# Weight sums made ahead that stand later on VectorE, and a last quarter of the down projection that makes its sums in place

## The chip, the cores and the metric

The kernel runs on one core of a Trainium2 chip. A core has a TensorE (PE) for matmuls, a VectorE (DVE) and a ScalarE (ACT) for elementwise work, a GpSimd (POOL), and a SyncE (SP) that issues most of the DMAs. The metric is the device time of one execution in microseconds (us); the time given is the median of several runs. A profile is one execution taken by the hardware profiler, whose times are a little longer than the median.

## The reference

One layer of a hybrid encoder on 512 tokens of width 2048, in float32:

```python
xn = _rmsnorm(h, norm_mix[l])
y = xn @ w_in[l]
o_gdn = _gdn_group(y[..., :GDN_COLS], ...)
o_rwkv = _rwkv_group(y[..., GDN_COLS:], ...)
h = h + concat([o_gdn, o_rwkv]) @ w_out[l]
h = h + _cross_attention(_rmsnorm(h, norm_xattn[l]), _rmsnorm(mem, norm_mem[l]), ...)
hn = _rmsnorm(h, norm_mlp[l])
h = h + jnp.square(jax.nn.relu(hn @ mlp_w_up[l])) @ mlp_w_down[l]
return _rmsnorm(h, norm_final)
```

The change concerns the last product, the down projection: 512 tokens, 8192 rows of weights, 2048 columns. Part of the change is also felt in the mixers (the two groups `gdn` and `rwkv`), because work for the down projection is done there as a filler.

## The kernel before, in words

**Stages.** In order of time: the input projection and the mixers (to about 1100 us), the output projection and the cross-attention (to about 1700), the up projection with 32 units (to about 2334), and the down projection with 8 units (to about 2944), then the last norm and the stores.

**Precision.** Every weight tile is cut in two by `cut` (line 1775): ScalarE copies it to a rounded half `whi`, VectorE subtracts to get the rest `wlo`. Three products of halves (high by high, low by high, high by low) replace one float32 product. There are three pairs of halves (`hfree`), so a cut can be at most three tiles ahead of the matmuls.

**Seven products for eight.** Output, up and down projections multiply 2 by 2 blocks with seven products instead of eight. Beside the four weight blocks A11, A12, A21, A22 that needs four sums: s1 = A21 + A22, s2 = s1 - A11, s3 = A11 - A21, s4 = A12 - s2. In the order of `order_of` (line 1803) a down unit multiplies A11 (product B11), A12 (B21), s2 (T2), s1 (T1), s3 (T3), s4 (B22) and A22 (T4). The right sides are blocks of the squared activations, made by `activations` (line 2131).

**Down.** A unit `("d", e, m)` has 2048 of the 8192 rows (e from 0 to 3) and one of two column groups (m). It runs the seven products, each over x = 0 to 3, that is four tiles of 128x1024; a tile is 12 matmuls of 512 columns. `downout` (line 2067) adds each finished product, for each of two token blocks t, from PSUM into the result rows `H`; two products into one bank follow each other only when the first has been added (the event "snap"). When e = 3, `final` (line 2164) follows: the squares for the last norm, and the product with its gain `wf`.

**Sums made ahead.** For the up projection the sums are made on the spot (`adds`). For down they are made ahead, in groups `(e, m)` of `GROUPS` (line 383), 16 in all, where e now counts 1024 rows: `presum` (line 391) loads a piece of the four blocks to four tiles, makes the four sums in place on VectorE, and stores each to DRAM (`Sd`). In the mixers, `presums` runs it in pieces of 410 columns on one set of four tiles `ds` (`NSET`, `PIECE`, `PRANK`, line 387) until the event `("kp", 15)`. What is left is done in chunks of 512 by `remaining` and `leftover` (lines 2191 and 2199): in up on the tiles of `abfree` until `("ud", 26, 1)`, and in down on the tiles of `cfree`. A group is 4 loads and 4 stores of a megabyte each, and later 4 more megabytes of loads of its sums. `loads` (line 1781) loads a down unit's tiles in the order of the products; a tile of a sum waits until its group is stored.

**Order.** The stages concerned are scheduled by hand. Generators (`chain`) yield one operation after another, and `run` (line 284) picks, again and again, the operation with the earliest planned start; 150 ns per rank are added to that start, so a lower rank goes first. The planned start comes from `start` and `issue`, which keep a clock for each engine, the planned time at which each buffer's last write lands (`landed`) and its last reader ends (`seen`). A DMA lands 2.9 us or more after its issue by the plan, plus a `margin` that a `Lane` carries (line 197). What is picked is written to that engine's program at once, so the plan sets the fixed order of every engine's program, and an engine runs its own program in that order whatever the real times are.

**Buffers.** `wfree` holds six tiles of 128x1024 for weights, three tagged `wraw` and three `w2` (shown as w in the profile). Two tiles `ws` and two `ab` (128x1024 each) serve the sums in up and the activations later (`abfree`, eight halves). `cfree` holds three tiles `sl` and the tile `acc`, 512 columns each. `hp` holds the residual; `hp[7]` is free once the last rows of `H` have been transposed (`norm_`, `turned_`, line 2059). `finals` (line 2211) loads the gain of the last norm, `nf`, into the two `ab` tiles when all activations have been made.

## Time and profile before

| | us |
|---|---|
| median of 3 runs | 2950.43 (2950.02 to 2954.77) |
| the profiled execution's own time | 2957.76 |
| its span, first to last instruction | 2955.7 |
| PE busy in the span | 2886.4 (98%) |
| DVE busy | 2317.0 (78%) |
| ACT busy | 1573.5 (53%) |
| mean granted clock of PE | 0.994 |
| moved by DMA | 587.64 MB, 199 GB/s on average |

A profile names an instruction by the line that issued it, its engine and operation, and by "out<-in" in the program's names, with buffer numbers left out. Almost all instructions of the stages concerned carry line 256, since `issue` emits them, so one goes by the names: `ds` is a piece of the sums made ahead in the mixers, `py` the input projection, `gn`, `ri..`, `gpo` and `gi..` are small matmuls of the mixers, `whi` and `wlo` the halves of a weight tile, `h` the result rows, `mxd`, `mmd`, `mgd`, `scrd`, `scgd` PSUM banks of down, `cb` the cut blocks of activations. Waits are written as "engine name <- engine name of what ended the wait: total us, times, longest us". Rows of stages give the stage, its length, and the busy time of each engine in it with the number of instructions. In the order of time, a row is start, duration, engine, instruction, and in brackets the idle time ahead of it and what ended it.

### The profile page before, as it was taken

To read this page: it belongs to the slowest core of one execution; us is meant where nothing else is said; L and a number is where in the kernel's file an instruction comes from. 1 tells how busy PE (TensorE), PEld (TensorE's weight loads), DVE (VectorE), ACT (ScalarE), POOL (GpSimd) and SP (SyncE) were. 2 spreads that over 40 slices of the span, in tenths; PEclk is the share of its full clock that TensorE was granted. 3 is DMA by queue.
4 is the path that set the end of the run, shared out by engine and by line. 5 is a ranking of instruction groups with operands and counts; after the bars stand their busy time and mean duration, and the time that the engine had idled before them with its cause. 6 is when DMAs were issued, how large, how long until landed. Compare 5 with 4: busy or idle time off the path is not lost. (4 is left out here: it accounts for less than half of the span.)

```text
span 2955.7 us, 49493 instructions
## 1 busy us (share of the span) xinstructions
PE 2886.4 (98%) x18794; PEld 2428.0 (82%) x18794; DVE 2317.0 (78%) x3559; ACT 1573.5 (53%) x2233; POOL 232.0 (8%) x547
## 2 busy tenths in 40 slices
PE   9999999999999999999999999999999999999998
PEld 7777777777777878888998888888888888888886
DVE  7787786877877876768975898888898878787865
ACT  7454544554555645565444656555555645454544
POOL 0213213122132200000000000000000000000000
PEclk9999999999999999999999999999999999999999
DMA  5756757667666778786433244555555778988755
GB/s 189 210 172 183 204 166 203 188 171 206 179 196 176 218 240 288 233 267 218 138 98 92 89 160 153 175 176 174 182 187 181 245 241 275 311 263 296 249 193 171
DMA packets 338206, 587.64 MB, mean 199 GB/s; under 512 B 103016, under 2 KB 202604, under 8 KB 337968
## 3 DMA queue, kind: packets, MB, share of 16 engines
q1 hardware_dynamic: 311728, 555.12, 61.0%
q10 hardware_dynamic: 26240, 29.37, 2.9%
q8 instruction: 147, 2.41, 0.3%
q14 instruction: 91, 0.75, 0.1%
HBM read 465.47 MB, written 118.89 MB: 198 GB/s over the span
## 5 line engine op out<-in xcount | busy, mean ns | idle before, releaser
L256 ACT CAST whi<-wraw 128x1024 fp32r<-128x1024 f32 (+1 forms) x374 | 392.0, 1049 | 423.1 <-PE py L256 147.4
L256 DVE TENSOR_TENSOR wlo<-wraw,whi 128x1024 fp32r<-128x1024 f32 (+1 forms) x374 | 459.3, 1229 | 113.9 <-ACT whi L256 104.1
L256 PE MATMUL py<-xhi,whi 128*128 128x512 f32 x928 | 374.1, 403 | 6.4 <-ACT xhi L256 6.4
L256 PE MATMUL py<-xlo,whi 128*128 128x512 f32 x928 | 378.2, 408 | 0.0
L256 PE MATMUL py<-xhi,wlo 128*128 128x512 f32 x928 | 376.5, 406 | 0.0
L256 ACT CAST whi<-w 128x1024 fp32r<-128x1024 f32 x190 | 200.1, 1054 | 222.7 <-PE mxu L256 47.4
L256 DVE TENSOR_TENSOR wlo<-w,whi 128x1024 fp32r<-128x1024 f32 x190 | 231.7, 1221 | 64.2 <-ACT whi L256 63.7
L256 PE MATMUL mxu<-cb,whi 128*128 128x512 f32 x1016 | 255.0, 392 | 0.0
L256 DVE TENSOR_TENSOR ds<-ds,ds 128x410 f32<-128x410 f32 (+1 forms) x228 | 134.3, 589 | 99.7 <-DMA ds<-in_w_dm 95.4
L256 PEld LDWEIGHTS py<-xhi,whi 128*128 128x128 f32 x928 | 177.0, 191 | 42.2 <-ACT xhi L256 6.4
L256 PEld LDWEIGHTS mxu<-cb,whi 128*128 128x128 f32 x1016 | 182.8, 189 | 32.7
L256 PEld LDWEIGHTS py<-xlo,whi 128*128 128x128 f32 x928 | 176.9, 191 | 36.4 <-DVE xlo L256 0.8
L256 PEld LDWEIGHTS py<-xhi,wlo 128*128 128x128 f32 x928 | 177.0, 191 | 33.5 <-issue 1.0
L131 DVE TENSOR_TENSOR wlo<-wraw,whi 128x1024 fp32r<-128x1024 f32 x112 | 136.7, 1222 | 45.1 <-ACT whi L130 44.0
L130 ACT CAST whi<-wraw 128x1024 fp32r<-128x1024 f32 x112 | 117.7, 1052 | 87.2 <-PE op L122 24.7
L256 PEld LDWEIGHTS mxu<-cb,wlo 128*128 128x128 f32 x1016 | 138.7, 190 | 10.5 <-DVE wlo L256 0.7
L256 PE MATMUL mxu<-cb,wlo 128*128 128x256 f32 x1016 | 142.2, 282 | 0.3 <-DVE wlo L256 0.3
L256 PE MATMUL mgu<-cb,whi 128*128 128x512 f32 x512 | 129.4, 394 | 1.8 <-ACT whi L256 1.8
L256 ACT ACT_TABLE_LOAD x87 | 111.6, 1283 | 36.6 <-DVE suml_gn L256 21.2
L256 PE MATMUL mxd<-whi,cb 128*128 128x512 f32 x512 | 126.8, 389 | 0.0
L256 PE MATMUL mgd<-whi,cb 128*128 128x512 f32 x512 | 126.4, 389 | 0.0
L122 PE MATMUL op<-ob,whi 128*128 128x256 f32 (+1 forms) x752 | 115.3, 304 | 0.3 <-ACT whi L130 0.3
(921 smaller groups left out, 6555.7 us busy)
## 6 DMA issues: line engine op xcount, KB each, us to landing
wraw<-in_w_in SPq DMA_DIRECT2D x116, 512.0 KB, 5.0
ds<-in_w_dm SPq DMA_DIRECT2D x184, 205.0 KB, 4.1
sd_s<-ds SPq DMA_DIRECT2D x184, 205.0 KB, 4.3
wraw<-in_w_up SPq DMA_DIRECT2D x65, 512.0 KB, 3.6
w<-sd_s SPq DMA_DIRECT2D x65, 512.0 KB, 5.0
w<-in_w_up SPq DMA_DIRECT2D x63, 512.0 KB, 4.1
wraw<-sd_s SPq DMA_DIRECT2D x63, 512.0 KB, 5.4
wraw<-in_w_dm SPq DMA_DIRECT2D x49, 512.0 KB, 4.8
```

Of the source, the lines that this page charges most:

```text
L122: PE.matmul(o, l, r, start=start, stop=stop, skip_group_check=again)
L130: S.copy(hi, src)
L131: V.tensor_tensor(out=lo, in0=src, in1=hi.bitcast(F32), op=ALU.subtract)
L256: f(*a, **k)
```

## The change

Three edits belong together. `presum` issues its loads through a lane with a margin of 5000 ns, and the filler's rank goes from 4 to 5. The four groups of the last quarter, `INSITU`, are no longer made ahead: `GROUPS` has 12 groups. The last quarter of down, e = 3, runs as four units of two x each instead of two units of four; their four blocks are loaded raw and a new generator `insitu` makes the sums in place in the load buffers, with one buffer more for s1. `splits`, `multiply_` and `downout` follow the shorter range `xs(u)`. To hold ten load buffers, `finals` hands the `ab` and `ws` tiles to `wfree` once the activations are done, and the gain `nf` goes to `hp[7]` and two tiles of `cfree` as four loads of 512 columns. What is left of the sums is in up also made on `hp[7]`, in chunks of 256 columns, until `("ud", 30, 1)`.

```diff
@@ -380,21 +380,23 @@
         wq += [("s", mem4[j]) for j in range(4) if n == NSQ[j]]
         wq += [("w", I["w_in"][n][:, h * 1024:(h + 1) * 1024]) for h in range(2)]
     kpo = [(0, 0), (1, 0), (0, 1), (1, 1)] + [(n, h) for n in range(2, KD) for h in range(2)]
-    GROUPS = [(e, m) for e in range(8) for m in range(2)]
+    INSITU = ((3, 0), (3, 1))
+    GROUPS = [(e, m) for e in range(8) for m in range(2) if (e // 2, m) not in INSITU]
     A11, A21, A22, A12 = range(4)
     Sd = {(e, m, j): pd.tile([P, 2048], F32, name=f"sd{e}_{m}_{j}", tag=f"sd{e}_{m}_{j}")
           for e, m in GROUPS for j in ("s1", "s2", "s3", "s4")}
-    NSET, PIECE, PRANK = 1, 410, 4
+    NSET, PIECE, PRANK = 1, 410, 5
     todo = list(GROUPS)
     upto = {}
 
     def presum(e, m, c, n, d, Q=None):
         Q = Q or SY
+        LD = Lane(nc.sync, "SP", margin=5000.0)
         tt = lambda o, a, b, op=ALU.subtract: DV.tensor_tensor(out=o, in0=a, in1=b, op=op)
         src = I["w_dm"][e, m]
         a11, a21, a22, a12 = b = [x[:, 0:n - c] for x in d]
         for i in (A21, A22, A11, A12):
-            yield Q.dma_start(b[i], src[i][:, c:n])
+            yield LD.dma_start(b[i], src[i][:, c:n])
         for j, op in (("s1", tt(a22, a21, a22, ALU.add)), ("s3", tt(a21, a11, a21)),
                       ("s2", tt(a11, a22, a11)), ("s4", tt(a12, a12, a11))):
             yield op
@@ -1750,6 +1752,7 @@
     wfree = [wraw() for _ in range(NWR)] + buffers(3, "w2")
     spare = pu.tile([P, T], F32, tag="spare", name="spare", bufs=1)
     sfree, abtiles = buffers(2, "ws"), buffers(2, "ab")
+    sfree_ = list(sfree)
     abfree, dfree = [abtiles[0][:, i * T:i * T + T] for i in range(2)], [abtiles[1]]
     parted.update((slot.get(x.tensor.name, x.tensor.name), 1) for x in abtiles + sfree)
     hfree = [wsplit() for _ in range(NWS)]
@@ -1776,17 +1779,28 @@
         yield AC.copy(hi, src)
         yield tt(lo, src, hi.bitcast(F32), ALU.subtract)
 
-    units = [("u", p, 0) for p in range(32)] + [("d", e, m) for e in range(4) for m in range(2)]
+    xs = lambda u: range(2 * u[3], 2 * u[3] + 2) if len(u) > 3 else range(4)
+    units = [("u", p, 0) for p in range(32)] + [("d", e, m, *y) for e in range(4) for m in range(2) for y in (((0,), (1,)) if (e, m) in INSITU else ((),))]
     raws, sums, halves = {}, {}, {}
     def loads():
         for u in units:
-            kind, e, m = u
+            kind, e, m = u[:3]
             if kind == "u":
                 src = I["w_up"][e]
                 for i in (A11, A12, A22, A21) if u == units[0] else (A11, A21, A22, A12):
                     raws[u, i] = r = yield from take(wfree)
                     yield SY.dma_start(r, src[i])
                     events.add(("raw", u, i))
+                continue
+            if (e, m) in INSITU:
+                for ws in (A11,), (A12,), (A21, "s1", A22):
+                    for x in xs(u):
+                        f, z = 2 * e + x // 2, x % 2
+                        for w in ws:
+                            raws[u, w, x] = r = yield from take(wfree)
+                            if w != "s1":
+                                yield SY.dma_start(r, I["w_dm"][f, m, w][:, z * 1024:z * 1024 + 1024])
+                                events.add(("raw", u, w, x))
                 continue
             for i, w in order_of(u):
                 for x in range(4):
@@ -1842,8 +1856,41 @@
             events.add(("sum", u, "s4"))
             release(u, "s2", sfree)
 
+    def insitu():
+        for u in units:
+            if u[0] != "d" or u[1:3] not in INSITU:
+                continue
+            for x in xs(u):
+                yield lambda: all(("raw", u, w, x) in events for w in (A11, A21, A22))
+                a11, a21, a22, s1 = (raws[u, w, x] for w in (A11, A21, A22, "s1"))
+                yield tt(s1, a21, a22)
+                events.add(("sum", u, "s1", x))
+                yield tt(a21, a11, a21, ALU.subtract)
+                events.add(("sum", u, "s3", x))
+                yield after("half", u, B11, x)
+                yield tt(a11, s1, a11, ALU.subtract)
+                events.add(("sum", u, "s2", x))
+            for x in xs(u):
+                yield after("half", u, B21, x)
+                a11, a12 = (raws[u, w, x] for w in (A11, A12))
+                yield tt(a12, a12, a11, ALU.subtract)
+                events.add(("sum", u, "s4", x))
+                yield after("half", u, T2, x)
+                wfree.append(a11)
+
     def splits():
         for u in units:
+            if u[0] == "d" and u[1:3] in INSITU:
+                for i, w in order_of(u):
+                    for x in xs(u):
+                        yield (after("sum", u, w, x) if isinstance(w, str) else after("raw", u, w, x))
+                        r = raws[u, {"s2": A11, "s3": A21, "s4": A12}.get(w, w), x]
+                        halves[u, i, x] = hl = yield from take(hfree)
+                        yield from cut(r, *hl)
+                        events.add(("half", u, i, x))
+                        if w not in (A11, A12, "s2"):
+                            wfree.append(r)
+                continue
             if u[0] == "d":
                 for i, w in order_of(u):
                     for x in range(4):
@@ -1872,7 +1919,7 @@
 
     def multiply_():
         for u in units:
-            kind, e, g = u
+            kind, e, g = u[:3]
             if kind == "d":
                 odd = units.index(u) % 2
                 tags = {B21: ("mm", "mm"), T1: ("mg", "mg"), B22: ("mg", "mg")}
@@ -1887,21 +1934,21 @@
                                 chain(downout(u, t, tag[0]), 0.2)
                     else:
                         yield lambda: all(("snap", u, {T2: B11, T3: T2, T4: T3, B22: T1}[i], t) in events for t in range(2))
-                    for x in range(4):
+                    for x in xs(u):
                         yield after("half", u, i, x)
                         yield after("block", e, i, x)
                         hi, lo = halves[u, i, x]
                         bh, bl = blocks[e, i, x]
-                        for ts in ((0,), (1,)) if u == units[-1] and i == T4 and x == 3 else ((0, 1),):
+                        for ts in ((0,), (1,)) if u == units[-1] and i == T4 and x == xs(u)[-1] else ((0, 1),):
                             for part, w_ in enumerate((hi, lo)):
                                 for t in ts:
                                     o = banks_of[u, tag[0], t][0]
                                     for kk in range(2):
                                         c, d = slice(kk * M + t * P, kk * M + t * P + P), slice(kk * 512, kk * 512 + 512)
-                                        yield mmr(o, bh[:, c], w_[:, d], fresh and x + part + kk == 0, stop=x == 3 and part + kk == 2)
+                                        yield mmr(o, bh[:, c], w_[:, d], fresh and x == xs(u)[0] and part + kk == 0, stop=x == xs(u)[-1] and part + kk == 2)
                                         if part == 0:
                                             yield mmr(o, bl[:, c], w_[:, d])
-                            if x == 3:
+                            if x == xs(u)[-1]:
                                 events.update(("mul", u, i, t) for t in ts)
                         hfree.append(halves[u, i, x])
                         if g == 1:
@@ -2065,7 +2112,7 @@
     two = lambda a: a.rearrange("p (q t) -> p q t", t=M)
 
     def downout(u, t, tag):
-        e, g = u[1:]
+        e, g = u[1:3]
         yield after("H", 3, 3)
 
         def add(m, half, src):
@@ -2082,7 +2129,7 @@
             events.add(("snap", u, i, t))
             if end:
                 events.add(kb)
-            if e == 3 and i in (B21, T3, B22, T4):
+            if e == 3 and u[3:] != (0,) and i in (B21, T3, B22, T4):
                 chain(final(2 * half + t, 2 * g + m), 2 if g == 0 else 1)
 
     ORDER = B11, B21, T2, T1, T3, B22, T4
@@ -2167,7 +2214,7 @@
         yield AC.activation(c, h, AF.Square, accum_out=cols5[t][:, g:g + 1])
         cfree.append(c)
         yield after("wf")
-        yield tt(h, h, wf[g // 2][:, g % 2 * 512:g % 2 * 512 + 512], ALU.mult)
+        yield tt(h, h, wf[g], ALU.mult)
         got[t] += 1
         if got[t] == 4:
             chain(store(t), 0.2)
@@ -2192,27 +2239,36 @@
         left = [(e, m, c, min(c + 512, 2048)) for e, m in todo for c in range(upto.get((e, m, "s4"), 0), 2048, 512)]
         yield after("xd", 7)
         chain(leftover(left, abfree, lambda d: True, after("ud", 26, 1)), lambda eng: 4)
+        yield after("H", 3, 3)
+        chain(leftover(left, [hp[7][:, i // 2, i % 2 * M:i % 2 * M + M] for i in range(4)], lambda d: True, after('ud', 30, 1), M), lambda eng: 4, ("spare7",))
+        yield after("spare7")
         yield after("mul", units[33], B11, 0)
         for n in range(1):
             chain(leftover(left, cfree if n == 0 else abfree, lambda d: phase() in (1, 2, 3, 5) or phase() >= d), lambda eng: 4)
 
-    def leftover(left, free, gate, stop=lambda: False):
+    def leftover(left, free, gate, stop=lambda: False, width=512):
         r = []
         for _ in range(4):
             r.append((yield from take(free)))
         while left and not stop():
             yield lambda: not left or gate(left[0][0] // 2 * 2 + left[0][1])
             if left:
-                yield from presum(*left.pop(0), r, SY)
+                e, m, c, n = left.pop(0)
+                for c in range(c, n, width):
+                    yield from presum(e, m, c, min(c + width, n), r, SY)
         free.extend(r)
 
     wf = []
 
     def finals():
         yield lambda: acts_done and len(abfree) == 8
-        for j in range(2):
-            wf.append(abtiles[j])
-            yield SY.dma_start(wf[j], I["nf"][:, j * 1024:j * 1024 + 1024])
+        wfree.extend(abtiles + sfree_)
+        yield after("spare7")
+        wf.extend((hp[7][:, 0], hp[7][:, 1]))
+        for _ in range(2):
+            wf.append((yield from take(cfree)))
+        for j in range(4):
+            yield SY.dma_start(wf[j], I["nf"][:, j * 512:j * 512 + 512])
         events.add(("wf",))
         for t in range(4):
             yield DV.scalar_tensor_tensor(out=cols5[t][:, 4:5], in0=q2[:, t:t + 1], scalar=2048 * 1e-6, in1=q2[:, t:t + 1],
@@ -2221,6 +2277,7 @@
 
     chain(loads(), 2)
     chain(adds(), 1.5)
+    chain(insitu(), 1.5)
     chain(splits(), 1)
     chain(multiply_(), 0)
     chain(abloads(), 3)
```

## Prediction

> **What bounds the kernel now.** I read the busy time by stage first, to see where TensorE (PE) is not full.
>
> ```profile
> 0.00:1100.00 1100.00, 1046.37 (x8982) 839.47 (x8983) 844.11 (x1567) 579.54 (x831) 231.97 (x547) 0.99 0.67 193
> 1400.00:1500.00 100.00, 100.00 (x734) 95.31 (x733) 94.05 (x127) 43.90 (x52) 0.00 (x0) 1.00 0.41 127
> 1700.00:2334.00 634.00, 631.91 (x3759) 561.41 (x3758) 561.45 (x739) 359.19 (x502) 0.00 (x0) 1.00 0.54 173
> 2334.00:2944.00 610.00, 610.00 (x2692) 504.54 (x2691) 463.64 (x554) 305.18 (x369) 0.00 (x0) 1.00 0.77 256
> 2944.00:2956.00 12.00, 0.04 (x1) 0.00 (x0) 4.02 (x11) 3.69 (x10) 0.00 (x0) 0.72 0.55 181
> ```
>
> The columns are length, then busy time of PE, its weight loads, VectorE (DVE), ScalarE, GpSimd, then granted clock, DMA share, GB/s. From 1700 on PE is full: 632 of 634 in up, 610 of 610 in down. Nothing that only relieves DVE or the DMA engines there can shorten the kernel. All the idle time worth having lies ahead of 1100, in the mixers: 1100 − 1046.4 = 53.6 us, and a granted clock of 0.99, which is another 1% of 1100 = 11 us (5.5 to 16.5 by rounding). So I read next what PE waits for there, and what DVE waits for.
>
> ```profile
> PE gn L256 <- DVE suml_gn L256: 18.7, 7, 4.7
> PE py L256 <- ACT xhi L256: 6.4, 1, 6.4
> PE gi6u L256 <- DVE gkn L256: 3.0, 1, 3.0
> PE gpo L256 <- DVE gE L256: 2.8, 1, 2.8
> PE ri1u L256 <- DVE k L256: 2.0, 1, 2.0
> PE ri5u L256 <- DVE k L256: 1.4, 1, 1.4
> PE ri2u L256 <- DVE k L256: 1.4, 1, 1.4
> ...
> DVE ds L256 <- DMA ds<-in_w_dm: 95.4, 36, 6.9
> DVE y L256 <- PE py L256: 29.0, 36, 3.6
> ```
>
> DVE's longest wait by far is for the loads of the weight sums made ahead (tile ds): 95.4 us in 36 waits, 2.65 us each, the longest 6.9. PE's waits for DVE in the rows shown make 18.7 + 3.0 + 2.8 + 2.0 + 1.4 + 1.4 = 29.3 us. Whether one causes the other is seen in the order of time around one of them (PE, then DVE):
>
> ```profile
> 241.10 0.39 PE L256 MATMUL py<-xhi,wlo 128*128 128x512 f32 x1
> 244.26 0.50 PE L256 MATMUL gn<-suml_gn,onesr 128*128 128x512 f32 x1 [2.77 <-DVE suml_gn L256]
> ...
> 238.40 1.13 DVE L256 SCALAR_TENSOR_TENSOR gE<-gE,RT,cst 128x128 f32<-128x128 f32 x4
> 243.01 0.59 DVE L256 TENSOR_TENSOR ds<-ds,ds 128x410 f32<-128x410 f32 x1 [3.49 <-DMA ds<-in_w_dm]
> 243.52 0.69 DVE L256 TENSOR_TENSOR suml_gn<-sg,sumh_gn 128x512 fp32r<-128x512 f32 x1
> ```
>
> DVE stands from 239.53 to 243.01 at a ds sum whose load has not landed. The suml_gn that PE needs is queued directly behind it, and PE stands for 2.77 us. This pattern, a filler with a late load in front of a critical instruction, is what I take the 29.3 us to consist of. A long wait has an aftermath:
>
> ```profile
> 481.09 0.50 PE L256 MATMUL gn<-suml_gn,onesr 128*128 128x512 f32 x1 [4.70 <-DVE suml_gn L256]
> 481.75 0.63 PE L256 MATMUL py<-xhi,whi 128*128 128x512 f32 x1
> 482.18 0.63 PE L256 MATMUL py<-xlo,whi 128*128 128x512 f32 x1
> 485.08 0.39 PE L256 MATMUL py<-xhi,wlo 128*128 128x512 f32 x1
> 485.31 0.39 PE L256 MATMUL py<-xhi,whi 128*128 128x512 f32 x1
> 481.00:486.00 5.00, 4.91 (x14) 3.91 (x15) 2.74 (x5) 3.88 (x4) 0.00 (x0) 0.66 1.14 230
> ```
>
> After 4.70 us of waiting, matmuls start 0.43 us apart instead of 0.23 and the granted clock over these 5 us is 0.66: (1 − 0.66) × 5 = 1.7 us more. The Trainium skill (TensorE: Matmul & The Clock Gate, section HAM oscillation) says the same: gaps of some 3.4 us drop the array to half clock until it has been busy for a window. The trace agrees at 481.
>
> **The change, part by part.**
>
> *Sums later in DVE's order, saves 28 us.* The planner is told that a ds load takes 5 us longer, and the rank goes from 4 to 5. It takes no instruction away; the four sums of a piece move behind others. 5 us is more than all but the longest of the 36 waits, so most of the 95.4 us should go, and the critical instructions behind them come on time. The pool is 29.3 us of waiting and 11 us of clock, 40 in all (the 6.4 us for xhi belong to the start and are not in it). Not all of the pool need be due to ds, and sums in a new order can meet other waits. I take seven tenths, 28 us. The lower bound is 5 (the waits move to another instruction), the upper is the pool.
>
> The stores move with the sums, and so do the next piece's loads, since there is one set of four ds tiles. Rows for the pace:
>
> ```profile
> L256 SPq DMA_DIRECT2D ds<-in_w_dm x228: 327/383/2667, 73.0 to 1088.1; - x114
> L256 SPq DMA_DIRECT2D ab<-in_w_dm x36: 327/424/1279, 1862.8 to 2220.6; - x36
> ```
>
> 228 loads are 57 pieces, one per 1015 / 57 = 17.8 us. Five us later each gives 22.8 at worst, 44 pieces. Twelve groups are 60 pieces, so 3 to 16 of them, at most 6560 columns or 13 chunks of 512, are left for up. Before, 9 such chunks (36 loads) stood in up on the ab tiles; the spare half of hp takes the rest in chunks of 256. At most four more chunks cost 4 × 4 × 0.60 = 10 us of DVE (0.60 from the rows further down; somewhat more in halves) over the 358 us of these loads. DVE was at 561/634 = 89% there; with 3% more it is still below the 94.05% of 1400 to 1500 with PE at 100.00. I count 0 (up to 3). In down the chunks on the sl tiles go: worth 0, since PE is full.
>
> *The last quarter's sums in place, costs 9 us.* The four groups no longer made ahead take 4 × 4 × 5 = 80 sums (at 410 columns) off the filler and 16 stores of a megabyte, and the last quarter loads 2 × 16 tiles instead of 2 × 28. DMA time is not what PE waits for in down, so this is worth 0. DVE gets 2 × 4 × 4 = 32 sums of 128x1024. As there are now four units of half the rows, each of the seven products is added to h twice as often: 28 more adds of 128x512. Prices:
>
> ```profile
> L256 DVE TENSOR_TENSOR wraw<-wraw,ws 128x1024 f32<-128x1024 f32 x16 | 19.5, 1219 | 0.3
> 2890.42 1.22 DVE L256 TENSOR_TENSOR wlo<-w,whi 128x1024 fp32r<-128x1024 f32 x1
> 2891.56 1.28 DVE L256 TENSOR_TENSOR h<-h,ab 128x512 f32<-128x512 f32 x2
> 2892.76 1.22 DVE L256 TENSOR_TENSOR wlo<-w,whi 128x1024 fp32r<-128x1024 f32 x1
> ...
> 2791.72 10.88 PE mxd L256 x48
> ...
> 2792.00:2868.00 76.00, 46.72 (x53) 1.00 0.64 207
> 2868.00:2956.00 88.00, 50.88 (x68) 0.96 0.53 173
> ```
>
> Back to back, a 1024 operation takes 2891.56 − 2890.42 = 1.14 us, a 512 add (2892.76 − 2891.56) / 2 = 0.60. That is 32 × 1.14 + 28 × 0.60 = 53.3 us. DVE was busy 46.72 + 50.88 − 4.02 (behind 2944) = 93.6 us in the quarter, which for PE lasts 2944 − 2791.7 = 152.3. It becomes 146.9 of 152.3, 96%. The highest share with PE at 100.00 is 94.05%: at it the quarter takes 156.2, **4 us** longer. At up's 88.6% it would be 165.8, 13.5 longer; if the plan fits all in, 0. I take 4, the nearest row.
>
> *The entry into the quarter.* A unit holds ten buffers: all six of the load pool and four tiles (ab, ws) that the activations' blocks give back last.
>
> ```profile
> 2790.89 0.90 SPq L256 DMA_DIRECT2D ab<-in_nf  x2
> 2793.64 0.68 DVE L256 TENSOR_TENSOR cb<-ws,cb 128x512 fp32r<-128x512 f32 x1
> L256 SPq DMA_DIRECT2D w<-in_w_dm x13: 327/328/333, 2762.4 to 2921.0; - x13
> DMA to landing us min/median/max: 3.1/4.8/8.9
> L256 ACT CAST whi<-w 128x1024 fp32r<-128x1024 f32 x55 | 58.0, 1055 | 76.0 <-PE mgd L256 21.1 <-PE mxd L256 20.6 <-PE scgd L256 14.6
> ```
>
> The first A22 can be loaded when an ab tile is free, about 2790.9 (now nf goes there), and lands about 2795.7; the second, in a ws tile, after 2794.3, landing about 2799.1. The third product needs s2 at 2791.7 + 2 × 2 × 2.72 = 2802.6 (48 matmuls take 10.88, a row of weights 2.72). Between lie six sums (6.8 us), the cuts of the second product (2.3), the adds of the first (1.2), and a cast of 1.06 ahead of PE: 2795.7 + 6.8 + 2.3 + 1.2 + 1.1 = 2807.1 for the second row, which is due at 2805.3, behind whatever the first is late. I take a wait of 3.5 us and half of the clock's aftermath, **4 us** in all. Bounds: 0 if the planner fills it well, 10 if a load lands in 8.9. In later units the last buffer comes free about two rows (5.4 us) before the unit ahead of it ends, its load takes 4.8, and its row of the third product is due 13.6 us into the unit: 14 us are left for three sums and a cut, 6 us of work, so I count no wait there. *The end* has one more short unit's finals on a fuller DVE: **1 us** (0 to 4).
>
> Sum: −28 + 0 + 4 + 4 + 1 = −19. The profiled run took 2957.76 us (span 2955.7), 7.3 above the median of 2950.43. 2957.76 − 19 = 2938.8; on the median's footing **2931**.
>
> **The rivals.** *Waits only change place.* The filler's loads come late because the stores ahead of them in the same four tiles do, and later sums make later stores: gain 5, loss 9, net +4, 2954. For it: the y row shows DVE also waits 29.0 us for PE; against it: 95.4 us is a filler's wait alone. *Slower, the last quarter becomes DVE's.* Mechanism: casts wait for PE to free a pair, DVE waits in order for the casts, and a 96% queue has no room for that. Price: at 88.6% 13.5, the entry at its 10, the end 4: 27.5. It decides from the point where this passes the gain: with a gain of 15, +12.5, 2963. For it: DVE waits for whi in every stage; against it: 1400 to 1500 at 94.05%. *More is won:* the whole pool of 40 and a smooth entry (loss 3) give −37, 2913. The Trainium skill (Perfetto Trace Analysis, section Identifying the Most-Contended Engine) judges by weight-load share rather than matmul share. *By rows alone:* the mixers have 839.47/1100 = 76%, down 504.54/610 = 83%; the mixers at 83% would be 85 us shorter, but many of their matmuls are small and the idle 53.6 us caps it, so it adds to this case only. *The change does not do what it says:* sums that are left over gate the loads of down's third quarter; at most 13 chunks at 40 us each on ab alone (1862 to 2220 for 9) end by 2380, ahead of 2639, so this is remote.
>
> **How the numbers follow.** Forecast 0.55 (own range 2918 to 2944), waits change place 0.15, slower 0.13, more won 0.15, the last 0.02. The time is the forecast's, 2931. The range, 2909 to 2955, leaves out the lower tail of the large gain and most of the slower case. A measurement tells 0.2% (5.9 us) from nothing: faster is below 2944.5, slower above 2956.3. Faster: 0.52 of the forecast, 0.15, and 0.06 of the second: 0.73. Slower: 0.12 and 0.02 of the rest: 0.14. Same: 0.13.
>
> **What would show it.** Right: DVE's wait for in_w_dm in the mixers well under 40 us, PE's wait gn for suml_gn under 8, the mixers' end some 28 us earlier; in the last quarter DVE above 90% busy and PE's only waits at its third product. Wrong: the ds wait gone and PE's idle time in the mixers unchanged (then ds was not the cause), or PE waiting for wlo or whi again and again in the last 150 us.

## The result, and the profile after

| | before | after |
|---|---|---|
| median of 4 runs, us | 2952.6 | 2930.32 (2927.78 to 2935.35) |
| ratio | | 0.9924 [0.9903, 0.9945] |
| profiled run, us (span) | 2957.76 (2955.7) | 2930.33 (2928.2) |
| mixers end (last matmul of kq) | 1176.9 | 1142.6 |
| up begins / down begins | 1696.2 / 2334.3 | 1662.9 / 2300.7 |
| last quarter begins / PE's last matmul | 2791.6 / 2943.7 | 2758.0 / 2914.2 |

The kernel became 22 us faster by medians, and the forecast was 2931. On the profiled runs the span fell by 27.5. The profiled run of before lay 5.2 above the median of its four runs, that of after on its median, which accounts for the difference. Against the medians of the kernel before in the later batches, 2954.7 to 2956.8, the gain is 24 to 26. The marks of the table say where: 34.3 us are won in the mixers, about 0.7 given back by the time down begins, 4.2 more in the last quarter (156.3 instead of 152.1) and 1.9 in the tail.

The busy time by stage, after, with the columns of the prediction's first view; then the same two stages of before, cut at the same events:

```profile
0.00:1142.60 1142.60, 1112.18 (x9418) 901.49 (x9419) 857.03 (x1566) 625.92 (x912) 225.44 (x547) 0.99 0.60 174
1700.00:2334.00 634.00, 632.58 (x3717) 560.53 (x3716) 564.47 (x744) 365.82 (x511) 0.00 (x0) 1.00 0.58 191
2758.00:2914.20 156.20, 153.21 (x672) 125.61 (x671) 143.28 (x164) 67.59 (x88) 0.00 (x0) 1.00 0.28 90
```

```profile
0.00:1176.90 1176.90, 1122.97 (x9418) 906.15 (x9419) 897.22 (x1650) 625.76 (x912) 231.97 (x547) 0.99 0.69 199
2791.60:2943.70 152.10, 152.10 (x673) 125.90 (x671) 93.98 (x110) 70.72 (x92) 0.00 (x0) 1.00 0.58 190
```

In the mixers PE runs the same 9418 matmuls. Its idle time falls from 1176.9 − 1123.0 = 53.9 us to 30.4, which is 23.5 us; the other 10.8 is less busy time for the same matmuls. Less half clock is only some 3 us of that: the granted clock, read in slices of 20 us, gives about 14 us lost to it in the mixers before and about 11 after. These views don't explain the remaining 7. In the last quarter DVE has 143.3 us to do instead of 94.0, 92% of it, and PE still waits only 3 us.

What PE waits for in the mixers after the change (total us, times, longest), to be held against the list of before:

```profile
PE ri6x L256 <- DMA r<-bg16T: 4.2, 2, 3.9
PE ri2x L256 <- DMA r<-bg16T: 3.2, 2, 3.0
PE ri5x L256 <- DMA r<-bg16T: 3.1, 2, 2.5
...
PE ri3x L256 <- DMA r<-bg16T: 2.1, 2, 1.6
PE ri4x L256 <- DMA r<-bg16T: 1.9, 2, 1.5
PE gn L256 <- DVE suml_gn L256: 1.5, 2, 1.1
```

The rows for r in that list of before:

```profile
PE ri7x L256 <- DMA r<-bg16T: 2.0, 2, 1.6
...
PE ri0x L256 <- DMA r<-bg16T: 1.9, 1, 1.9
...
PE ri5x L256 <- DMA r<-bg16T: 0.9, 2, 0.7
...
PE ri6x L256 <- DMA r<-bg16T: 0.6, 2, 0.3
```

The wait gn for suml_gn went from 18.7 us to 1.5, and the waits gi6u, gpo, ri1u, ri2u, ri5u are gone. A new one has come: the loads of r from bg16T hold PE for 4.2 + 3.2 + 3.1 + 2.1 + 1.9 = 14.5 us, where the four rows of before made 2.0 + 1.9 + 0.9 + 0.6 = 5.4. Over all rows of the two lists, PE's waits for DVE fall from 39.2 us to 2.6, those for loads rise from 6.2 to 16.9, and those for ScalarE from 7.2 to 9.6; together that is the 23.5 us of idle time. The filler's own tile, after:

```profile
L256 SPq DMA_DIRECT2D ds<-in_w_dm x144: 327/401/2219, 74.1 to 1050.3; - x144
L256 DVE TENSOR_TENSOR ds<-ds,ds x144: 567/580/2149, 105.9 to 1076.5; 128x410 f32<-128x410 f32 x116, 128x408 f32<-128x408 f32 x28
```

144 loads are 36 pieces instead of 57. No row of DVE's waits in the mixers names these loads any more: the 95.4 us of waiting are gone.

### The profile page after: what moved, and what is told of

Its sections match the earlier page's. It is cut to its first block, busy times and chain, and to the rows that moved or that the text cites. A ratio compares the mean times of both kernels' runs of the same rounds, so it can differ in the third digit from the quotient of the medians.

```text
span 2928.2 us, 49166 instructions
## 1 busy us (share of the span) xinstructions
PE 2877.8 (98%) x18794; PEld 2422.9 (83%) x18794; DVE 2331.5 (80%) x3551; ACT 1572.7 (54%) x2233; POOL 225.4 (8%) x547
## 5 line engine op out<-in xcount | busy, mean ns | idle before, releaser
L256 ACT CAST whi<-wraw 128x1024 fp32r<-128x1024 f32 (+1 forms) x364 | 381.6, 1049 | 436.8 <-PE py L256 163.2
L256 DVE TENSOR_TENSOR wlo<-wraw,whi 128x1024 fp32r<-128x1024 f32 (+1 forms) x364 | 446.3, 1227 | 114.6 <-ACT whi L256 102.9
L256 ACT CAST whi<-w 128x1024 fp32r<-128x1024 f32 x181 | 190.5, 1054 | 220.0 <-PE mxu L256 47.3
L256 DVE TENSOR_TENSOR wlo<-w,whi 128x1024 fp32r<-128x1024 f32 x181 | 220.7, 1221 | 50.5 <-ACT whi L256 49.1
L256 PEld LDWEIGHTS mxd<-whi,cb 128*128 128x128 f32 x512 | 95.8, 188 | 23.7 <-ACT whi L256 3.5
```

Of the source, the lines that this page charges most:

```text
L256: f(*a, **k)
```

## The experiments

The theory is that of the prediction: a ds sum whose load is late stands in DVE's order in front of a critical instruction, and the margin moves it behind. Against it stand: that it is the number of sums, thus DVE's work, or the DMA traffic that counts; that the waits only change place; and, for the quarter's entry, that a late A22 is the cause. Each ran beside the kernel before on the same chip, whose median was 2954.7 to 2956.8 in these batches. "Mixers end" and "pieces" are from each run's profile.

| kernel | us | ratio to before | mixers end | pieces | DVE waits for ds, us | last quarter |
|---|---|---|---|---|---|---|
| margin and rank alone (e1) | 3060.1 | 1.0361 [1.0346, 1.0377] | 1141.6 | 36 | none | waits |
| in place alone (e2) | 2961.9 | 1.0027 [1.0016, 1.0038] | 1175.4 | 57 | 97.4 | 157.4 |
| after, rank 4 (e3) | 2925.1 | 0.9900 [0.9885, 0.9915] | 1137.4 | 41 | none | 156.3 |
| after, no margin (e4) | 2953.1 | 0.9988 [0.9976, 1.0000] | 1162.2 | 47 | 54.4 | 157.4 |
| after, margin 2500 (e5) | 2956.6 | 1.0008 [0.9999, 1.0018] | 1172.0 | 41 | 11.6 | 157.4 |
| after, pieces paced (e6) | 2920.5 | 0.9886 [0.9869, 0.9902] | 1135.4 | 37 | 29.1 | 157.4 |
| after, r loads' lane (e7) | 2912.9 | 0.9861 [0.9846, 0.9875] | 1120.6 | 40 | 5.3 | 157.4 |
| after, entry's loads (e8) | 2928.8 | 0.9916 [0.9899, 0.9932] | 1141.8 | 36 | none | 157.7 |
| no late loads (e9) | 2976.2 | 1.0066 [1.0046, 1.0086] | 1198.2 | 57 | none | 152.1 |
| narrow sums (e10) | 2948.8 | 0.9974 [0.9957, 0.9991] | 1168.0 | 57 | 102.5 | 152.1 |
| e7 and e8 together (e11) | 2914.6 | 0.9855 [0.9840, 0.9869] | 1123.6 | 40 | 8.1 | 160.5 |
| e7, rank 4 (e12) | 2953.4 | 0.9988 [0.9978, 0.9997] | 1166.2 | 41 | 2.3 | 157.4 |

### The two halves of the change, each alone

The first takes the margin and the rank into the kernel before, whose 16 groups all have their sums made ahead:

```diff
-    NSET, PIECE, PRANK = 1, 410, 4
+    NSET, PIECE, PRANK = 1, 410, 5
...
+        LD = Lane(nc.sync, "SP", margin=5000.0)
...
-            yield Q.dma_start(b[i], src[i][:, c:n])
+            yield LD.dma_start(b[i], src[i][:, c:n])
```

> The kernel before with the margin of 5000 ns and rank 5 alone: all 16 groups are made ahead, the last quarter is as before. Theory (a late load in front of a critical instruction): the mixers end near 1143 us instead of 1177, VectorE's wait for in_w_dm in ds goes from 95 us to under 10. About 36 pieces are made there, so 8.8 groups are left over; if down gets them in time the whole is some 34 us faster (about 2918), if they are late down pays it back in waits for sums and the whole is 2920 to 2990. Rival (the fewer groups matter): the mixers gain less than half, since there is as much left to make.

The mixers won all that they won in the changed kernel (1141.6), and down lost 104 us more than that. A stage of its down projection, and the waits of PE and of ScalarE's casts from 2300 on:

```profile
2742.00:3046.00 304.00, 204.46 (x872) 167.62 (x870) 176.94 (x223) 96.97 (x125) 0.00 (x0) 0.83 0.72 240
```

```profile
PE mxd L256 <- ACT whi L256: 101.0, 3, 66.0
ACT whi L256 <- DMA wraw<-sd_s: 91.4, 5, 72.1
...
ACT whi L256 <- DMA w<-sd_s: 52.1, 7, 34.9
```

PE is busy 204 of 304 us there. 36 pieces instead of 57 leave 27 chunks of sums for down, whose loads run until 2983; the casts of the later units wait for the sums (sd_s) to come back from memory, up to 72 us, and PE for the casts. The direction was expected, the price far underestimated. The second keeps the quarter in place and undoes the margin and the rank:

```diff
-    NSET, PIECE, PRANK = 1, 410, 5
+    NSET, PIECE, PRANK = 1, 410, 4
...
-        LD = Lane(nc.sync, "SP", margin=5000.0)
+        LD = Lane(nc.sync, "SP", margin=0.0)
```

> The changed kernel with margin 0 and rank 4: 12 groups, last quarter in place. Theory: the mixers end near 1177 as before, 57 pieces and 95 us of waits in ds; last quarter 156 us and an end of 14, so 5 to 7 us slower than before (about 2957). Rival (the smaller amount of sums brings the gain): a gain of 20 us or more remains, below 2935.

As the theory has it: 57 pieces, and in the mixers the waits of before:

```profile
DVE ds L256 <- DMA ds<-in_w_dm: 97.4, 40, 7.8
```

```profile
PE gn L256 <- DVE suml_gn L256: 21.2, 7, 5.7
```

The in-place quarter costs some 6 us by itself and brings nothing. The two parts are worth +104 and +6 us apart and −22 together: the margin makes the gain, and the quarter in place removes the sums that then cannot be made in time.

### The margin and the rank

From the changed kernel, first only the rank back to 4, then only the margin back to 0, then half a margin:

```diff
-    NSET, PIECE, PRANK = 1, 410, 5
+    NSET, PIECE, PRANK = 1, 410, 4
```

> The changed kernel with the margin but rank 4. Theory: the margin does it, so within 8 us of the changed kernel (2922 to 2938), ds waits under 10 us. Rival (the rank does it): the mixers end near 1170.

```diff
-        LD = Lane(nc.sync, "SP", margin=5000.0)
+        LD = Lane(nc.sync, "SP", margin=0.0)
```

> The changed kernel with rank 5 but margin 0. Theory: rank is 150 ns in the plan against waits of 2.65 us, so it changes little: mixers' end 1165 to 1180, ds waits over 60 us, 2945 to 2960. Rival (the rank does it): mixers' end near 1143, about 2930.

```diff
-        LD = Lane(nc.sync, "SP", margin=5000.0)
+        LD = Lane(nc.sync, "SP", margin=2500.0)
```

> The changed kernel with a margin of 2500 ns. The mean wait in ds was 2.65 us, the longest 6.9, so by the theory about half of the gain: ds waits 15 to 45 us, mixers' end 1150 to 1165, 2937 to 2952. Rival (any delay of the filler does, or the number of pieces): mixers' end within 5 us of 1143.

With the margin the rank is not needed: at rank 4 the mixers end at 1137.4, and PE has no wait for r there. The rank without the margin takes DVE's waits from 97.4 to 54.4 us and brings 1175.4 − 1162.2 = 13 us in the mixers and 9 us of time against the in-place quarter alone. The margin brings 37 us of time without the rank (2961.9 to 2925.1) and some 20 with it (23 by the medians, which are of different batches, 19 by the ratios): the two overlap, and the margin is the larger.

The half margin missed what was expected (1150 to 1165): DVE's waits for ds are nearly gone, yet the mixers end at 1172.0. Its waits of PE, and the stretch in which the time is lost:

```profile
PE ri6x L256 <- DMA r<-bg16T: 9.6, 1, 9.6
...
PE ri7s L256 <- DVE k L256: 4.3, 1, 4.3
PE ri5u L256 <- DVE k L256: 3.4, 1, 3.4
```

```profile
820.00:880.00 60.00, 42.47 (x445) 32.73 (x444) 38.13 (x80) 25.84 (x43) 15.74 (x36) 0.80 0.60 168
```

In these 60 us alone PE is idle 17.5, and a granted clock of 0.80 takes more. Four of the remaining ds waits (4.4, 2.5, 1.2 and 0.9 us) stand at 819 to 834, ahead of one head's chain of k and r. This kernel has as many pieces (41) as the one at rank 4 and loses 34.6 us of mixers against it. So neither the number of pieces nor the sum of the ds waits gives the mixers' end. Whether these four waits made that head late is taken up below.

### Pacing, DVE's work and the loads

The first holds each piece back until a given matmul group has run, without any margin:

```diff
+                paced.append(1)
+                k = 3 + len(paced) * 8 // 5
+                yield lambda: k > 58 or ("py", k) in events or stop()
...
-        LD = Lane(nc.sync, "SP", margin=5000.0)
+        LD = Lane(nc.sync, "SP", margin=0.0)
```

> The changed kernel with margin 0, rank 5, and each piece of the mixers held back until a given input projection is done, so that about 35 pieces are made at an even pace, as many as in the changed kernel, but with the loads' time in the plan as before. Theory (order, not amount): waits in ds stay at some 2.6 us for more than half of the pieces, 45 us or more in all, and the mixers end at 1155 or later. Rival (the amount of VectorE work and DMA in the mixers): mixers' end near 1143.

```profile
DVE ds L256 <- DMA ds<-in_w_dm: 29.1, 14, 5.9
```

```profile
PE gn L256 <- DVE suml_gn L256: 2.5, 4, 1.7
```

The theory expected at least 45 us of ds waits and no end before 1155; it got 29.1 and 1135.4. Pieces that don't follow one another on the one set of tiles have less late loads to begin with, and pacing does as much as the margin. What it shares with the changed kernel is the lower rate of loads (176 and 174 GB/s in the mixers, 199 before). The half margin has the rate too (177) and gained nothing, so the rate is not enough, but how much of the gain is its doing is not settled by these runs.

The next keeps the order, the loads and the stores of the kernel before, and makes the mixers' sums on 8 columns only; the rest of the sums made there is left out:

```diff
+            k = op[4]
-            yield op
+            yield op[:4] + ({**k, **{z: k[z][:, 0:8] for z in ("out", "in0", "in1")}},) + op[5:] if x_ds(d) else op
```

> The kernel before with the same order and the same loads, waits and stores, but the mixers' sums done on 8 of their columns; most of these sums are left out so, the result is not the reference's. That takes some 57 x 4 x 0.45 = 100 us of VectorE work out of the mixers. Theory: the waits for the loads stay, so the mixers end within 12 us of 1177 (1165 or later) and gn <- suml_gn stays above 12 us. Rival (the amount): mixers' end near 1145.

```profile
0.00:1168.00 1168.00, 1121.04 (x9417) 906.31 (x9418) 803.50 (x1650) 626.20 (x912) 218.47 (x547) 0.99 0.69 200
```

```profile
DVE ds L256 <- DMA ds<-in_w_dm: 102.5, 42, 6.5
```

DVE's work falls by 897.2 − 803.5 = 93.7 us, more than twice the 40 that the change takes off, and the mixers win 9 us of the 34. The waits remain. The order of the instructions is that of before, so no new plan blurs this: the amount of work explains about a quarter of the gain.

The last takes the lateness away instead: the loads go to a scratch in memory that nothing reads, and the sums read a constant tile, so that the sums made ahead are left out:

```diff
-            yield Q.dma_start(b[i], src[i][:, c:n])
+            op = Q.dma_start(b[i], src[i][:, c:n])
+            yield op[:3] + ((scratch[i][:, 0:n - c], src[i][:, c:n]),) + op[4:] if x_ds(d) else op
...
-            yield op
+            r = cst[:, 576:576 + n - c]
+            yield op[:4] + ({**op[4], "in0": r, "in1": r},) + op[5:] if x_ds(d) else op
```

> The kernel before with the same order on every engine, but the loads of the mixers' pieces go to a scratch tensor in DRAM and the sums there read a constant tile, so that no sum can wait for its load; the amount of VectorE work, the number of DMAs and the bytes read stay. The sums made ahead are left out so, the result is not the reference's. Theory (late loads ahead of critical work): VectorE's 95 us of waits in ds go, TensorE's gn <- suml_gn falls from 18.7 to under 5 us, the mixers end 25 to 40 us earlier (1137 to 1152 instead of 1177). Rival (amount of work, or 36 pieces instead of 57): the mixers end above 1165.

```profile
PE ri5x L256 <- DMA r<-bg16T: 7.3, 2, 7.1
PE ri1x L256 <- DMA r<-bg16T: 6.6, 1, 6.6
...
PE ri2x L256 <- DMA r<-bg16T: 5.6, 1, 5.6
...
PE gn L256 <- DVE suml_gn L256: 2.7, 3, 1.4
```

The wait gn fell from 18.7 to 2.7 us, as the theory has it: the late loads in DVE's order were its cause. But the mixers end at 1198.2 instead of the 1137 to 1152 expected, since the r loads took over with 38 us of waits in all heads, and the loads of lw with 9.9. The experiment is confounded: its copies write to memory as well, and by the profile's table of transfers they land after a median of 6.7 us where the ds loads took 4.1. It shows the cause of the gn wait and which wait stands behind it, not how many us the late loads cost.

### The wait that came in its place

The r loads are on a lane whose margin was 2500; here it is 5000, on top of the change:

```diff
-    SL, SM = Lane(nc.sync, "SP", wait=6000.0), Lane(nc.sync, "SP", margin=2500.0)
+    SL, SM = Lane(nc.sync, "SP", wait=6000.0), Lane(nc.sync, "SP", margin=5000.0)
```

> The changed kernel with the lane of the loads of r, E and lw (bg16T, bg16U, bg8, w2a2) at a margin of 5000 ns instead of 2500. After the change TensorE's longest waits in the mixers are for r<-bg16T, 14.5 us, with half-clock stretches behind them. Theory: the same cure applies, so the matmuls that use r stand later among the input projection's and these waits fall under 5 us: 8 to 18 us faster than the changed kernel (2912 to 2922). Rival: the chain of one head behind them is itself what ends last, so the wait turns up further on: within 4 us of 2930, or slower.

```profile
0.00:1120.60 1120.60, 1104.38 (x9418) 895.33 (x9419) 870.73 (x1582) 624.91 (x912) 225.41 (x547) 1.00 0.63 183
```

```profile
PE ri7s L256 <- DVE k L256: 2.7, 1, 2.7
PE gn L256 <- DVE suml_gn L256: 2.6, 3, 1.1
```

All waits for r are gone, PE's idle time falls from 30.4 to 16.2 us, and the granted clock is 1.00. **At 2912.9 us this version beats both kernels**: the same cure, applied to the wait that had taken the first one's place, brings another 17 us.

How far this rests on one plan shows when the same kernel goes back to rank 4:

```diff
-    NSET, PIECE, PRANK = 1, 410, 5
+    NSET, PIECE, PRANK = 1, 410, 4
```

> e7_inverse_margin with rank 4 instead of 5. With the margin, rank 4 was some 5 us faster than rank 5 in the changed kernel. If that adds up, 2905 to 2910; if it was only another arrangement of the same waits, which e7 has none of, within 5 us of 2913.

```profile
820.00:880.00 60.00, 43.94 (x424) 35.07 (x420) 40.30 (x83) 25.33 (x40) 19.87 (x46) 0.77 0.54 145
```

```profile
PE ri6x L256 <- DMA r<-bg16T: 6.3, 2, 6.1
...
PE ri5u L256 <- DVE k L256: 5.0, 1, 5.0
```

All expectations missed. The mixers end 46 us later than at rank 5, and 820 to 880 looks like that of the half margin: PE idle for 16 us and a clock of 0.77. DVE's ds waits are 2.3 us in the whole of the mixers here, so this head can be late without them, and the four waits seen at the half margin are not shown to be its cause there. The traces show where the lateness sits. What PE waits for is the end of a chain: GpSimd works on the tile sr of this head, the result is stored to bg16T, and r is loaded from there. In this kernel GpSimd begins at 810.8 us, 135 after its start on the head before, and at the half margin at 816.1, 134 after, where the kernel at rank 5 (e7) has 115. The head was thus set back before its r load was issued (828.0 and 834.4), which a margin on that load doesn't cure. What set it back stays open.

### The entry into the last quarter

After the change, PE's waits from 2700 on, and PE around the first unit's third product (T2, the second mxd):

```profile
PE mxd L256 <- ACT whi L256: 2.6, 2, 2.4
PE mxd L256 <- DVE wlo L256: 0.2, 1, 0.2
```

```profile
2757.98 1.98 PE L256 MATMUL mxd<-whi,cb 128*128 128x512 f32 x8
...
2775.18 2.11 PE L256 MATMUL mxd<-whi,cb 128*128 128x512 f32 x8 [2.35 <-ACT whi L256]
2777.43 1.20 PE L256 MATMUL mxd<-wlo,cb 128*128 128x512 f32 x4
2778.46 1.75 PE L256 MATMUL mgd<-whi,cb 128*128 128x512 f32 x7
```

Three products are six rows of 2.72 us, 16.3; they took 2778.46 − 2757.98 = 20.5. These 4.2 us are the whole loss of the quarter: PE has no other wait until its last matmul. What DVE does before the cast that PE waits for:

```profile
2763.17 0.69 DVE L256 TENSOR_TENSOR rstd<-rstd,mxd 128x512 f32<-128x512 f32 x1 [0.58 <-PE mxd L256]
...
2764.37 1.22 DVE L256 TENSOR_TENSOR wraw<-wraw,ab 128x1024 f32<-128x1024 f32 x1
...
2771.49 1.22 DVE L256 TENSOR_TENSOR ab<-w,ab 128x1024 f32<-128x1024 f32 x1
2772.74 1.22 DVE L256 TENSOR_TENSOR w<-ws,w 128x1024 f32<-128x1024 f32 x1
```

From 2763.17 to 2773.96 DVE works without a gap. The second row's s2 (w from ws and w) is the eleventh operation of that stretch; its cast takes 1.05 us and PE goes on at 2775.18. No load is waited for, and DVE is busy for 20.3 of the 22 us from 2752 to 2774. To see whether the loads' order had put the sums there, the first row's loads were set ahead of A12:

```diff
-                for ws in (A11,), (A12,), (A21, "s1", A22):
-                    for x in xs(u):
+                y0, y1 = xs(u)
+                for ws, ys_ in ((A11,), (y0, y1)), ((A21, "s1", A22), (y0,)), ((A12,), (y0, y1)), ((A21, "s1", A22), (y1,)):
+                    for x in ys_:
```

> The changed kernel with the last quarter's loads in another order: A21, the buffer for s1 and A22 of the first row ahead of A12, so that the first row's sums need none of the four late buffers. Theory: the 4.1 us that TensorE loses at the third product of the first in-place unit (2.6 of them waits for whi) come from the late A22; they fall to 0 to 2 us, the quarter from 156.3 to 152 to 154.5, and the whole is 2 to 4 us faster. Rival (VectorE's six sums in a row are the cause, whatever the loads): still 3 us or more at that place.

```profile
2755.19 1.98 PE L256 MATMUL mxd<-whi,cb 128*128 128x512 f32 x8
...
2772.64 3.50 PE L256 MATMUL mxd<-whi,cb 128*128 128x512 f32 x8 [2.33 <-ACT whi L256]
```

```profile
2761.83 1.22 DVE L256 TENSOR_TENSOR w<-w,wraw 128x1024 f32<-128x1024 f32 x1
```

```profile
2758.27 1.05 ACT L256 CAST whi<-ab 128x1024 fp32r<-128x1024 f32 x1 [2.21 <-DMA ab<-in_w_dm]
```

The first row's last load is issued by 2749.2 here, 6 us before the quarter begins; in the changed kernel it goes to an ab tile at about 2755, 3 us before. Yet the first sum starts 6.6 us into the quarter (2761.83 − 2755.19), no earlier than the 6.4 after the change (2764.37 − 2757.98), and PE's wait is as long. The experiment is not clean, because now A12 is what comes late: ScalarE's cast of it waits 2.21 us for its load, and DVE 1.25 us for that cast. The in-place kernel without the margin (e2) tells the same without this flaw: its last load for the first unit is issued 3.2 us into the quarter instead of 0.4 ahead of it, and PE's wait is 2.36 us, as long as in the changed kernel. So late loads of A22 are not the cause; DVE's cuts and adds, which stand ahead of the sums, are what these traces show. Together with the longer lane margin and an earlier rank for the sums:

```diff
-    chain(insitu(), 1.5)
+    chain(insitu(), 1.1)
```

> e7_inverse_margin with the loads' order of e8_entry_order and the in-place sums at rank 1.1 instead of 1.5, that is ahead of the last blocks of activations and behind the cuts. In e8 the first row's data came early and TensorE lost as much at the third product; if it is VectorE's order there (sums behind everything else), the last quarter falls from 157.4 to 154 to 156 us and the whole is 2 to 4 us faster than e7 (about 2910). Rival (the six sums do not fit in any order): 157 us, as e7.

The quarter took 160.5 instead of the 154 to 156 expected, with a wait of 4.0 us at the third product and one of 1.3 at the second, where the cast of A12 waits 3.9 us for its load. The time was that of the kernel without it. No order tried removes the wait. Fewer operations at the entry were not tried.

## Why the prediction was right

- **What bounds the kernel** held. Up took 637.8 us instead of 638.1, and all that was won was won ahead of it.
- **Sums later in DVE's order, 28 us.** The mechanism was right: the margin takes the waits away (e3, e4), the gn wait goes with the lateness of the loads (e9), DVE's work explains some 9 us of it (e10), and fewer loads alone do not do it (e5). What each part is worth in us is known only as well as neighbouring plans agree, and e5 and e12 show that a plan can lose 30 us for a reason of its own. The size was 34.3 on the profiled runs, inside the 40 of the pool, but it is made up in another way, so that 28 came near is in part luck. The pool's 29.3 us took six rows of PE's waits for DVE; the whole list had 39.2, of which 36.6 went. Of the 11 us of clock only some 3 came back. New waits for loads and for ScalarE took 13.1, and some 7 us of the gain are not explained. If the 5.2 us by which the profiled run of before lay above its median belong to its mixers, it is 29; the traces can't tell.
- **The pace, "44 pieces at worst", was wrong.** By the rows of the two traces a piece's first sum came 11.0 us (median) after its first load instead of 5.75, which is the margin and little more. The term that failed is the rank, which the prediction put at nothing: with the margin at rank 4 there were 41 pieces (e3), near the 44, and rank 5 takes 10 pieces off without the margin (57 in e2, 47 in e4) and 5 with it, so that 36 were made. It cost nothing in time, as the chunks left over ran in up and down, where PE is full all the same; but "in down the sl chunks go" was wrong as well:

```profile
L256 SPq DMA_DIRECT2D sl<-in_w_dm x24: 327/422/515, 2387.6 to 2658.0; - x24
```

  With the 8 loads on acc, 8 chunks stay in down, 10 before. The rival of sums that gate down, taken as remote, decided the margin alone (e1): without the quarter in place the leftover is 27 chunks and costs over 100 us.
- **The last quarter, DVE saturated, 4 us: measured 0.** DVE at 92% had room enough; PE waited only at the entry, where DVE worked without a gap. The quarter of before ran with DVE at 62%, so there was no row between, and 94.05% at a full PE was no limit but only the highest share that the trace had.
- **The entry, 4 us: measured 4.2**, at the product named, and the size is luck. Of its working only the DVE part holds; "A22 late" was wrong (e2, e8). Its own sum gave 2807.1 − 2805.3 = 1.8 us and took 3.5, and the half clock that it counted behind the wait didn't come in this run.
- **The end, 1 us: measured 1.9.** DVE is busy for 6.4 us behind the last matmul instead of 4.0.
- **The sum.** −28 + 0 + 4 + 4 + 1 = −19 against −33.6 + 4.2 + 1.9 = −27.5 on the profiled runs, and −22.3 on medians (−20 from the median known ahead). The 4 us too much for DVE and the gain that was taken low point the same way, so on the profiled runs the forecast was 8.5 us short; by medians it came out this close because the median that it started from was a low one.
- **The rivals.** "Waits only change place" was half true: 14.5 us of waits for r came up, and removing them gave 2912.9 (e7), about the time of the rival that more is won. The slower rival did not come: its price, 13.5 us at 88.6%, was of the saturation that was not there.

## What to carry to other kernels

An engine that runs its program in order pays for a filler's late load in whatever stands behind it (18.7 us of PE's waits for one tile here), so a planner should count on the late landing time for filler loads and for those of the critical chain, and the first thing to read is the instruction queued behind the wait. Filler that is moved later needs a place where it still fits: the margin without the quarter in place lost 104 us. Neighbouring plans differ by more than the effect looked for (1120.6 and 1166.2 for the mixers with one rank changed), so one part is best judged by its waits and not by the time of a single plan.

## What was not expected of the hardware

A wait of PE of the same length can halve the clock or leave it alone. The granted clock in the four us that hold the end of the 2.35 us wait of the changed kernel, and of the 2.33 us wait of the kernel with the entry's loads in another order:

```profile
2775.00:2779.00 4.00, 3.68 (x15) 2.74 (x16) 4.00 (x5) 3.08 (x4) 0.00 (x0) 1.00 0.49 155
```

```profile
2773.00:2777.00 4.00, 4.00 (x12) 3.16 (x11) 3.15 (x4) 2.30 (x3) 0.00 (x0) 0.58 0.63 196
```

The eight matmuls behind the wait took 2.11 us in the one and 3.50 in the other. In the second, PE had also been idle for 0.55 us one row of matmuls earlier, where it was 0.30 in the first. That is not what decides: the kernel with the r loads' longer margin (e7) had 0.30 there too, and its matmuls are slowed all the same:

```profile
2751.58 2.79 PE L256 MATMUL mxd<-whi,cb 128*128 128x512 f32 x8 [2.35 <-ACT whi L256]
```

Of the eight kernels with this same last quarter, two kept the clock (the changed kernel and e3, 156.3 us) and six did not (e2, e4 to e7 and e12, 157.4). Each was profiled once, so whether it changes from run to run is not known. The Trainium skill (TensorE: Matmul & The Clock Gate, section HAM oscillation) has idle gaps above some 3.4 us as the rule; the second trace does not agree, since 2.33 us sufficed there. What decides it these runs don't show. So the price of a short wait has two values, 2.3 us and 1.1 to 1.4 more.
